# Keeping two engines in written order through the first block of seven products, with parameters, angles and the forget chain placed behind it

## The chip, the core and the metric

The kernel runs on one core of one Trainium2 chip. The metric is the device time of one execution in microseconds (us); smaller is better. An execution has five engines at work: TensorE (PE: matmuls, and PEld for its weight loads), VectorE (DVE), ScalarE (ACT), GpSimd (POOL) and SyncE (SP, which here only issues DMA transfers). Each engine carries out its own list of instructions in the order of the list and waits where an operand, a buffer or a transfer is not ready. Which instruction stands where in a list is therefore part of the program.

## What is computed

The reference is one decoder block on a sequence of 512 tokens and a width of 1024. One wide projection feeds two branches (an mLSTM matrix memory with 4 heads of 256, and a sparse attention with 8 heads of 64); their outputs are projected, merged by gates and projected once more.

```python
hN = _rmsnorm(x, norm_g[l])
p = _split_in(hN @ w_in[l])                      # 1024 x 8992, columns split by name
mq = silu(_causal_dwconv(p["m_q"], conv_q_w[l], conv_q_b[l]))
mk = silu(_causal_dwconv(p["m_k"], conv_k_w[l], conv_k_b[l]))
mh = _mlstm(mq, mk, p["m_v"], p["m_i"] + b_igate[l], p["m_f"] + b_fgate[l])
ya = sigmoid(p["m_o"]) * _head_layernorm(mh, mh_norm_g[l]) * silu(p["m_z"])
yn = _nsa(...)                                   # uses rope angles, compressed keys, gates
yb = yn * silu(p["n_z"])
merged = sigmoid(p["g_a"]) * (ya @ w_branch_a[l]) + sigmoid(p["g_b"]) * (yb @ w_branch_b[l])
x = x + merged @ w_out[l]
return _rmsnorm(x, final_norm_g)
```

The part that matters here is the early one: the columns `m_v`, `m_o` and `m_z` of the projection (1024 x 1024 each), the first columns of `g_a` and `g_b`, the small vectors (convolution weights, positions, compression positions), the rope angles (cosine and sine of the positions) and the logarithm of the forget gate.

## The kernel before

Every fp32 matmul is done in three fp32r matmuls: an operand is split into a high part (ACT, `A(hi, src, AF.Copy)`) and a low part (DVE, `lo = src - hi`), and the products hi·hi, hi·lo and lo·hi are added in PSUM. A split of one 128 x 1024 tile is one ACT pass and one DVE pass. All ACT and DVE instructions go through a helper and carry its line, L79, so they are told apart by tile names.

**Start.** The 512 tokens are normalised, transposed and split in four blocks of 128 into `hTh` and `hTl`. Each block is multiplied by a small set of columns (`last`, matmuls of L160 to L162), whose results `evacuate` takes out (`vsw`, `gp`).

**Seven products.** `winograd` computes a 1024 x 1024 projection in seven block products P1 to P7 rather than eight. A product is 24 matmuls of 128 x 512 (L482). The token side needs sums of blocks of `hTh + hTl`, which `token_sums` forms on DVE in the buffer `gate` and splits into the operands `S1` to `S4` (`S2h` and `S2l` for instance are the high and low part of `S2`). The weight side needs sums of quarter weights (`plus`: tiles `T`, from the loaded quarters `R`) and their splits (`hilo`: tiles `wh` and `wl`, four buffers each, handed from one split to the next when the matmuls that read them are done). The order of the products is P1, P2, P6, P7, P4, P5, P3. Results wait in `ka`, `kz`, `kw` (ACT copies) and are added on DVE by `finish` into the tiles `cq`. The block is run three times: for the columns `m_v`, `m_o` and `m_z`. `winograd` takes a table `between` of functions that are called after a named product.

**Jobs.** Between the products stand jobs of the `stream` object: 24 matmuls each (L202, L204, L206) that project 128 columns of `g_a` or `g_b`; ACT evacuates each into `sg`. In the first block four jobs run (J1 to J4 below). In the built order of before, J1 and J2 lie in among P1 and P2, J3 and J4 follow, then P6.

**Order.** The names in the set `ordered` are the engines whose instructions keep the order in which the code is written. The set holds ACT and DVE at the start, and `ordered.clear()` empties it right behind the evacuation of the fourth token block. From there on a scheduler places ACT and DVE instructions. Matmuls and transposes on PE are placed by the scheduler throughout.

**What stands behind `ordered.clear()`.** First the parameters (L398 to L417): eight small loads and one of 516 KB (`cst`), one POOL pass (`rotR`), and ten short PE transposes of `rows`, `crow` and `pf` into one bank, copied out by DVE as `prm`, `cpos` and the positions. Then the first `winograd` with `between` = one job and one step of `token_sums` after P1, three jobs and two steps after P2, and `angles` after P4. The function `angles` holds the angles (tiles `tiny`, a sine on ACT that needs its own table load, `cpad` and `spad`, eight PE transposes of L609 into `Ct` and `St`), the branch gates and the forget chain: a row of some 20 DVE instructions of 128 x 16 elements on `tiny`, each on the result of the one before, that ends in `lf` and `lfs`.

## Time and profile before

| what | value |
|---|---|
| time, median of 3 runs | 644.49 us (643.85 to 645.53) |
| the profiled execution's own time | 644.23 us |
| its span, first to last instruction | 642.4 us |
| PE busy | 613.9 us, 96% |
| DVE busy | 474.8 us, 74% |
| ACT busy | 335.4 us, 52% |
| mean granted TensorE clock | 0.991 |

The profile shows one execution. A row of the timeline gives the start and the length in us, the engine, the line, the operation, out<-in by tile names, and in square brackets the idle time of the engine just before, with the instruction that ended it. A row of the windows gives for a stretch A:B its length, and then for each engine the busy time and the number of instructions, the granted clock (1.00 is full speed), the share of time in which the DMA engines were busy, and GB/s. Matmul lengths overlap, since matmuls are pipelined: what one costs is the distance from one start to the next.

### The profile page before, as it was taken

What the parts mean: (1) busy time and instruction counts of PE and PEld (TensorE: products, weight loads), DVE (VectorE), ACT (ScalarE), POOL (GpSimd) and SP (SyncE); (2) the same over time, 40 slices, a digit from 0 to 9 for tenths busy, and PEclk for the clock granted to TensorE, in tenths of its full rate; (3) what the DMA queues carried; (4) which work ended last, traced back from release to release, by engine and by line L of the source; (5) the groups of instructions that cost most, each with busy time, mean ns of one, the idle gap of its engine ahead of it and who ended that gap; (6) DMA issues with size and microseconds to landing.
All of it is one profiled execution on the core that took longest, in us unless ns stands there. A gap on an engine that the chain in (4) does not pass through costs nothing.

```text
span 642.4 us, 8937 instructions
## 1 busy us (share of the span) xinstructions
PE 613.9 (96%) x3206; PEld 515.7 (80%) x3206; DVE 474.8 (74%) x938; ACT 335.4 (52%) x642; POOL 51.4 (8%) x114
## 2 busy tenths in 40 slices
PE   5977999999999999999999999999999999999995
PEld 3965887888888878887878877888888878888995
DVE  4999648779677577886876777789898987556444
ACT  5652554565443256566566575565656563234234
POOL 4100000000000002121212212000000000000000
PEclk9997999999999999999999999999999999999999
DMA  7942633622029453133032311622323254843103
GB/s 228 345 119 74 205 109 123 196 66 57 25 82 244 112 128 83 50 82 89 21 105 62 88 55 42 187 79 66 98 67 99 65 148 125 290 140 95 56 2 131
DMA packets 83659, 71.30 MB, mean 111 GB/s; under 512 B 4720, under 2 KB 68372, under 8 KB 83616
## 3 DMA queue, kind: packets, MB, share of 16 engines
q1 hardware_dynamic: 83616, 70.75, 37.0%
q8 instruction: 25, 0.41, 0.3%
q14 instruction: 18, 0.15, 0.1%
HBM read 61.30 MB, written 8.39 MB: 108 GB/s over the span
## 4 chain that ended last, share of the span: by engine, by line
PE 74%; DVE 16%; ACT 4%; issue 2%; DMA 2%; POOL 1%; SPq 0%; DVEq 0%; POOLq 0%; ACTq 0%
PE pp L204 12%; PE pp L202 12%; PE pp L206 12%; PE ps L482 9%; PE pt L482 4%; PE pp L162 3%; PE pp L482 3%; PE pp L161 3%; PE pp L160 3%; DVE wl L79 3%; DVE u L79 3%; PE pt L939 2%; PE po L952 1%; PE po L951 1%; ACT wh L79 1%
## 5 line engine op out<-in xcount | busy, mean ns | idle before, releaser
L202 PE MATMUL pp<-hTh,wh 128*128 128x512 f32 (+1 forms) x360 | 142.9, 397 | 0.0
L204 PE MATMUL pp<-hTl,wh 128*128 128x512 f32 (+1 forms) x360 | 140.3, 390 | 0.0
L206 PE MATMUL pp<-hTh,wl 128*128 128x512 f32 (+1 forms) x360 | 140.2, 389 | 0.0
L79 ACT ACTIVATE wh<-wr 128x1024 fp32r<-128x1024 f32 x64 | 67.5, 1058 | 75.4 <-PE pp L204 59.4
L79 DVE TENSOR_TENSOR wl<-wr,wh 128x1024 fp32r<-128x1024 f32 x64 | 77.9, 1218 | 14.1 <-ACT wh L79 14.1
L206 PEld LDWEIGHTS pp<-hTh,wl 128*128 128x128 f32 x360 | 67.9, 189 | 13.1
L202 PEld LDWEIGHTS pp<-hTh,wh 128*128 128x128 f32 x360 | 68.0, 189 | 10.5
L204 PEld LDWEIGHTS pp<-hTl,wh 128*128 128x128 f32 x360 | 68.1, 189 | 9.8
L933 POOL TENSOR_SCALAR P<-P,st 128x128 f32<-128x128 f32 (+1 forms) x64 | 34.4, 557 | 160.9 <-DVE st L79 69.0
L79 DVE TENSOR_TENSOR wl<-T,wh 128x1024 fp32r<-128x1024 f32 x24 | 29.3, 1223 | 19.9 <-ACT wh L79 19.9
L79 ACT ACTIVATE P<-P,st 128x128 f32<-128x128 f32 (+3 forms) x64 | 35.5, 556 | 11.2 <-DVE st L79 10.7
L79 DVE TENSOR_TENSOR ptl<-pt,pth 128x512 fp32r<-128x512 f32 (+1 forms) x64 | 29.9, 485 | 14.1 <-ACT pth L79 13.7
L79 ACT ACTIVATE pth<-pt 128x512 fp32r<-128x512 f32 (+1 forms) x64 | 26.9, 434 | 25.9 <-PE pt L939 14.5
L79 DVE CUSTOM_DVE_ANT_0 P<-ps,cst 128x128 f32<-128x128 f32 (+3 forms) x64 | 30.5, 487 | 12.7 <-PE ps L925 12.4
L161 PE MATMUL pp<-wl,meh 128*128 128x256 f32 x128 | 36.2, 283 | 0.0
L160 PE MATMUL pp<-wh,meh 128*128 128x256 f32 x128 | 36.2, 283 | 0.0
L162 PE MATMUL pp<-wh,mel 128*128 128x256 f32 x128 | 36.2, 284 | 0.0
L79 DVE SCALAR_TENSOR_TENSOR u<-pp,prm,u 128x511 f32<-128x511 f32 (+2 forms) x48 | 35.7, 744 | 0.2
L79 ACT ACTIVATE wh<-T 128x1024 fp32r<-128x1024 f32 x24 | 25.3, 1058 | 17.4 <-PE pp L204 6.5
L939 PE MATMUL pt<-cst,P 128*128 128x128 f32 x160 | 28.4, 277 | 0.9 <-DVE ptl L79 0.7
L939 PEld LDWEIGHTS pt<-cst,P 128*128 128x128 f32 x160 | 19.8, 141 | 10.8 <-DVE ptl L79 5.8
L79 DVE TENSOR_TENSOR wl<-R,wh 128x1024 fp32r<-128x1024 f32 x18 | 21.7, 1220 | 8.4 <-ACT wh L79 8.3
(324 smaller groups left out, 1410.9 us busy)
## 6 DMA issues: line engine op xcount, KB each, us to landing
wr<-w_in SPq DMA_DIRECT2D x44, 512.0 KB, 4.0
R<-w_in SPq DMA_DIRECT2D x24, 512.0 KB, 4.2
gD<-sg SPq DMA_DIRECT2D x16, 256.0 KB, 2.2
s<-gD SPq DMA_DIRECT2D x16, 256.0 KB, 5.2
wr<-w_branch_a SPq DMA_DIRECT2D x8, 512.0 KB, 3.8
wr<-w_out SPq DMA_DIRECT2D x8, 512.0 KB, 3.7
vD<-cq SPq DMA_DIRECT2D x8, 256.0 KB, 3.0
wr<-vD SPq DMA_DIRECT2D x4, 512.0 KB, 4.8
```

The costliest lines, as they stand in the source:

```text
L79: ins = fn(*args, **kw)
L160: pe.matmul(ps, a, c, start=start and i == 0, stop=False)
L161: pe.matmul(ps, a, d, start=False, stop=False)
L162: pe.matmul(ps, b, c, start=False, stop=stop and i == n - 1)
L202: pe.matmul(ps, a, c, start=k == 0, stop=False)
L204: pe.matmul(ps, a, d, start=False, stop=False)
L206: pe.matmul(ps, b, c, start=False, stop=k == nk - 1)
L482: m = lambda l, r, first=False, last=False: pe.matmul(banks[tb], l, r, start=first, stop=last, skip_group_check=True)
L933: pool.tensor_scalar(pj, pj, st[:, 2, j : j + 1], 1.0, OP.mult, OP.mult)
L939: pe.transpose(pt[:, (qb - kb) * 128 : (qb - kb) * 128 + 128], P[:, POFF[qb] + kb * 128 : POFF[qb] + kb * 128 + 128], ident,)
L951: pe.matmul(po[:, kb * 128 :], vl, th[:, :n], start=False, stop=False)
L952: pe.matmul(po[:, kb * 128 :], vl, tl[:, :n], start=False, stop=b == 1 and kb == 3)
```

## The change

The set `ordered` is no longer emptied behind the start but after P6 of the first block, so that ACT and DVE keep the written order through most of it, and the code is written in the order wanted. `hilo` moves out of `winograd`, and the weight split for P1 (`w1`) is written ahead of the first job's. The jobs and steps of the first block are called at new places of `winograd` (`t3`, `t2`, `C11`, `w6` beside the product names). The parameters become a generator `params`: its first part issues the loads, after the sum `t2`; its second part (the POOL pass, the transposes, the copies) runs after P7. Its tiles move: `rows` into the buffer `zt` of the third block, `crow` and `pi` into a wider `tiny`. `zt` is one tile of two halves where it was two buffers. `token_sums` forms its fourth sum one step earlier. `angles` stays behind P4. What is computed is the same.

```diff
         vq = quarters(vview, ((0, 0), (1, 0)))
+        w1 = hilo(vq[0, 0])
         stream.fetch()
         vq.update(quarters(vview, ((0, 1), (1, 1))))
         evacuate(NT - 1, last)
-        ordered.clear()
-
-        nc.sync.dma_start(cst[:, CROT:], consts[:, CROT:])
...
-        dve.tensor_copy(posT, ps[:, 128:132])
...
         t(c, b, c, OP.subtract)
+        t(d, c, hl("A12")[0], OP.add)
+        t(d, d, hl("A12")[1], OP.add)
         yield
         split(c, *parts["S2"])
         split(a, *parts["S3"])
         yield
-        t(d, c, hl("A12")[0], OP.add)
-        t(d, d, hl("A12")[1], OP.add)
         split(b, *parts["S1"])
         split(d, *parts["S4"])
...
-        product("P1", X, "A11", hilo(b11))
+        product("P1", X, "A11", w1 or hilo(b11))
+        do("P1")
         a = keep(X, "ka")
         Z = [PP() for _ in range(2)]
         w2 = hilo(b21)
         t3 = plus(WS(), b12, b22)
+        do("t3")
         t2 = plus(WS(), t3, b11)
+        do("t2")
         product("P2", Z, "A12", w2)
+        do("P2")
         finish(0, 0, Z, a, OP.add)
-        product("P6", X, "S2", hilo(t2), False)
+        do("C11")
+        w6 = hilo(t2)
+        do("w6")
+        product("P6", X, "S2", w6, False)
+        do("P6")
...
+    def params():
+        nc.sync.dma_start(cst[:, CROT:], consts[:, CROT:])
+        rows = wn.tile([128, D], F32, name="zt", tag="zt")[:11]
+        crow = tiny[:32, 384:512]
+        pi = tiny[:4, 512:640].bitcast(I32)
+        nc.sync.dma_start(pi, positions[0].rearrange("(a b) -> a b", a=4))
...
+        yield
+        pool.tensor_scalar(rotR, cst[:, CROT : CROT + 128], 1.0, 1.0, OP.mult, OP.mult)
+        ps = PP()
+        for k in range(8):
+            pe.transpose(ps[:, k * 11 : (k + 1) * 11], rows[:, k * 128 : (k + 1) * 128], ident[:11, :11])
...
+        pf = tiny[:4, 0:128]
+        dve.tensor_copy(pf, pi)
...
-    winograd(vq, staged, v_out, {"P1": (job, step), "P2": (job, step, job, step, job), "P4": (angles,)})
+    more = params()
+    load = lambda: next(more)
+    winograd(vq, staged, v_out, {
+        "P1": (step,), "t3": (job,), "t2": (job, load), "P2": (step,), "C11": (job, step),
+        "w6": (job,), "P6": (ordered.clear,), "P7": (lambda: next(more, None),), "P4": (angles,),
+    }, w1)
```

The built order shows what becomes of this. On PE the first block reads P1, J1, J2, P2, J3, J4, P6, P7, the parameter transposes, P4, P5 after the change. On ACT the copies `ka` and the split `wh` of P2 follow at once on P1; the sine and its table load, which stood ahead of P6's evacuation, stand between the two `wh` splits for P3.

DVE, from the end of the forget chain to the low split of P2's weights, before (`lf`, `lfs`: end of the chain; `prm`, `cpos`, `tiny`: parameters; `T`: weight sums; `wl<-wr`: a job's low split; `wl<-R`: P2's):

```order
L79 SCALAR_TENSOR_TENSOR lf<-gp,tiny 128x16
L79 TENSOR_TENSOR lfs<-lfs,lf 128x4 x2
L79 COPY prm<-pt 128x88
L79 COPY cpos<-pt 128x32
L79 TENSOR_SCALAR prm<-prm 128x8
L79 COPY tiny<-pt 128x4
L79 TENSOR_TENSOR T<-R 128x1024 x2
L79 TENSOR_TENSOR T<-T,R 128x1024
L79 TENSOR_TENSOR wl<-wr,wh 128x1024
L79 TENSOR_TENSOR wl<-R,wh 128x1024 x2
```

The same place now, from the last token sum (`gate`) on:

```order
L79 TENSOR_TENSOR gate<-gate,hTl 128x1024
L79 TENSOR_TENSOR wl<-R,wh 128x1024 x2
L79 TENSOR_TENSOR T<-R 128x1024 x2
L79 TENSOR_TENSOR wl<-wr,wh 128x1024
L79 TENSOR_TENSOR T<-T,R 128x1024 x2
L79 TENSOR_TENSOR wl<-wr,wh 128x1024
L79 TENSOR_TENSOR S2l<-gate,S2h 128x1024
L79 TENSOR_TENSOR S3l<-gate,S3h 128x1024
L79 TENSOR_TENSOR cq<-pp,ka 128x512 x2
L79 TENSOR_TENSOR tiny<-tiny 128x16
```

P2's low split stands right behind the token sums; eleven instructions of the forget chain follow only behind `cq`, still ahead of `S1l`, `S4l` and the low split for P6, and the rest of the chain comes later. Two of the eight sums on `gate`, which stood in among the token blocks of the start, are now in the row ahead of this place, and so is the cast of the loaded positions (`CAST tiny<-tiny 4x128`).

DVE at the end of the block, where the copies into `cpad` and `spad` (`cq<-tiny`) stand, and the results of P5 (`cq<-pt,kw`) are taken out. Before:

```order
L79 TENSOR_TENSOR wl<-R,wh 128x1024 x2
L79 TENSOR_TENSOR T<-R 128x1024
L79 TENSOR_TENSOR cq<-pt,kw 128x512
L79 TENSOR_TENSOR wl<-R,wh 128x1024
L79 TENSOR_TENSOR cq<-pt,kw 128x512
```

The same place now:

```order
L79 TENSOR_TENSOR wl<-R,wh 128x1024
L79 COPY cq<-tiny 128x4x8 x8
L79 TENSOR_TENSOR wl<-R,wh 128x1024
L79 TENSOR_TENSOR T<-R 128x1024
L79 TENSOR_TENSOR wl<-R,wh 128x1024
L79 TENSOR_TENSOR T<-R 128x1024
L79 TENSOR_TENSOR cq<-pt,kw 128x512 x2
```

Two sums `T<-R` of the second block, on freshly loaded quarters, now both stand ahead of `cq<-pt,kw`, and a low split of the second block between them.

PE at the same place, after P5 (`S1h`, `S1l`) and up to P3 (`S4h`, `S4l`); `ps` is the bank of the second block's P1. Before:

```order
L482 MATMUL pt<-wl,S1h 128x512
L482 MATMUL pt<-wh,S1l 128x512
L482 MATMUL pt<-wh,S4h 128x512
L482 MATMUL pt<-wl,S4h 128x512
L482 MATMUL pt<-wh,S4l 128x512
```

The same place now:

```order
L458 MATMUL pt<-wh,S1l 128x512
L458 MATMUL ps<-wh,hTh 128x512 x2
L458 MATMUL ps<-wl,hTh 128x512
L458 MATMUL ps<-wh,hTl 128x512
L458 MATMUL ps<-wh,hTh 128x512
L458 MATMUL ps<-wl,hTh 128x512
L458 MATMUL ps<-wh,hTl 128x512
L458 MATMUL ps<-wh,hTh 128x512
L458 MATMUL ps<-wl,hTh 128x512
L458 MATMUL ps<-wh,hTl 128x512
L458 MATMUL pt<-wh,S4h 128x512
```

Ten matmuls of the second block's P1 now stand ahead of the first block's P3. The eight transposes of L609 (`cq`), which stood between P4 and P5, stand after the ninth matmul of P5.

## The prediction

> **What bounds the kernel now.** I read the busy shares first, then the waits of PE, then the windows around the longest of them, and last the timelines of the two engines waited for.

> ```profile
> PE 613.9 (96%) x3206; PEld 515.7 (80%) x3206; DVE 474.8 (74%) x938; ACT 335.4 (52%) x642; POOL 51.4 (8%) x114
> PE pp L482 <- DVE wl L79: 4.0, 1, 4.0
> PE pp L482 <- ACT wh L79: 3.8, 1, 3.8
> PE pp L162 <- DVE hTl L79: 0.2, 1, 0.2
> PE ps L303 <- DMA grow<-norm_g: 4.5, 1, 4.5
> ```

> PE is busy for 96% of the span, so the end moves only by what PE waits or runs slowly. Two of its longest waits are single ones in the first block of products, both of P2, for the high and the low split of its weights.

> ```profile
> 30.81:41.74 10.93, 10.93 (x50) 8.77 (x48) 10.93 (x20) 3.92 (x8) 0.88 (x1) 1.00 0.31 91
> 41.74:46.39 4.65, 0.86 (x11) 0.69 (x10) 4.03 (x20) 4.46 (x7) 0.00 (x0) 1.00 0.62 165
> 46.39:52.81 6.42, 2.39 (x5) 1.38 (x5) 6.39 (x11) 3.73 (x4) 0.00 (x0) 0.51 0.33 87
> 52.81:56.39 3.58, 3.58 (x9) 2.81 (x9) 3.58 (x4) 0.00 (x0) 0.00 (x0) 0.50 0.56 148
> ...
> 41.51 0.39 PE L206 MATMUL pp<-hTh,wl 128*128 128x512 f32 x1
> 59.80 0.39 PE L202 MATMUL pp<-hTh,wh 128*128 128x512 f32 x1
> 75.44 0.39 PE L482 MATMUL ps<-wh,S2h 128*128 128x512 f32 x1
> ```

> Behind the first wait the granted clock (the column after POOL) falls to 0.51 and stays at 0.50 up to 56.39. From 59.80 to 75.44 lie 69 matmuls (the 21 left of J2, J3, J4): 15.64 / 69 = 0.2267 us each. J1 and P1 end at 41.51 + 0.23 = 41.74, and P6 begins at 75.44. Between lie P2, J2, J3 and J4, 96 matmuls or 21.76 us, in 33.70 us: **11.94 us are lost there**, by waiting and by the slow clock. That is all that this change can win at this place.

> ```profile
> 41.94 0.60 ACT L79 ACTIVATE sg<-pp 128x512 f32<-128x512 f32 x1 [7.14 <-PE pp L206]
> 43.38 1.07 ACT L79 ACTIVATE S2h<-gate 128x1024 fp32r<-128x1024 f32 x1
> 45.27 2.01 ACT L79 ACTIVATE wh<-R 128x1024 fp32r<-128x1024 f32 x2
> ...
> 42.67 0.17 DVE L79 TENSOR_SCALAR tiny<-tiny 128x16 f32<-128x16 f32 x1
> 42.88 0.18 DVE L79 TENSOR_TENSOR tiny<-tiny 128x16 f32<-128x16 f32 x1
> 46.99 2.36 DVE L79 TENSOR_TENSOR T<-R 128x1024 f32<-128x1024 f32 x2
> 51.54 2.35 DVE L79 TENSOR_TENSOR wl<-R,wh 128x1024 fp32r<-128x1024 f32 x2
> ```

> ACT was idle for 7.14 us until J1 ended, and then did `sg`, `ka`, `S2h` and a job's split before P2's `wh` at 45.27. DVE stood in the forget chain from 42.67 on (0.21 from one instruction to the next), then the parameters' copies and the sums `T`, before P2's `wl` at 51.54. Neither engine lacked time; both did other things first.

> **The change, part by part.** All times below are in the clock of this execution.

> PE up to P6: P1 can start at 30.81, where J1 started, if its split is ready.

> ```profile
> 28.61 2.00 ACT L79 ACTIVATE wh<-wr 128x1024 fp32r<-128x1024 f32 x2
> 33.78 1.21 DVE L79 TENSOR_TENSOR wl<-R,wh 128x1024 fp32r<-128x1024 f32 x1
> 34.92 1.31 DVE L79 TENSOR_TENSOR gate<-gate,hTh 128x1024 f32<-128x1024 f32 x1
> 62.00 1.28 DVE L79 TENSOR_TENSOR cq<-pp,ka 128x512 f32<-128x512 f32 x2
> ```

> ACT's first two splits run at 28.61 to 30.61, a DVE pass is 34.92 - 33.78 = 1.14 us, so P1's low splits end near 30.8 and 32.0; P1 needs them at 31.0 and 32.4. Then J1, J2, P2, J3, J4 follow without a break if DVE and ACT keep up: P2 at 30.81 + 72 x 0.2267 = 47.13, P6 at 30.81 + 144 x 0.2267 = 63.46.

> Does DVE keep up? Before, it came to its token sums at 34.92, behind four low splits and the last token block's small copies. The same stand ahead of them now, the splits in another order and the first not before ACT's at 29.7: I take 35.1. To P2's first low split stand eight sums, six small instructions (0.8 together, less than the 0.21 of the rows above for each, since they stand among passes and not on each other's results) and the pass itself: 35.1 + 9 x 1.14 + 0.8 = 46.2; P2's second matmul needs it at 47.4. Margin 1.2. To P6's second low split: 22 passes (25.1), the small ones (0.8), two `cq` (1.28), eleven of the forget chain (11 x 0.21 = 2.3): 35.1 + 29.5 = 64.6; needed by P6's eighth matmul at 65.05. Its first is done at 63.4 and needed at 63.69. Margin 0.3. So the forecast's wait here is 0; DVE 5% slower (1.5 us over this row) would cost 1.2. ACT has time: `wh` of P2 follows `ka` at 36.3 and is done near 39.5, and the three evacuations `sg` ahead of other splits cost 0.6 each where ACT waits for the job anyway.

> The loads: the positions that DVE casts now come behind a job's weights, which wait for the third low split (33.0), and `cst`.

> ```profile
> 25.72 0.41 SPq L402 DMA_DIRECT2D pi<-positions  x1
> 34.28 0.88 POOL L410 TENSOR_SCALAR rotR<-cst 128x128 fp32r<-128x128 f32 x1 [11.27 <-DMA cst<-consts]
> crow<-cmp_pos_k SPq DMA_DIRECT2D x1, 8.0 KB, 8.4
> ```

> SP issues them near 34.4. With ten large loads ahead, `cst` landed at 34.28 and `crow` took 8.4; now only two are ahead. By 8.4 they would land at 42.8, against the cast at 41.4: 1.4 late, of which P2's margin takes 1.2, but P6's only 0.3, so up to 1.1. By the load's median below (4.2) they are in time. I take 0, since the queue ahead is short.

> The parameter transposes move from a stretch in which PE waited anyway to a gap-free one between P7 and P4. Their cost was hidden; now it is open:

> ```profile
> 41.83 0.66 PE L413 MATMUL pt<-cst,rows 11*128 11x11 f32 x8
> 42.41 0.20 PE L417 MATMUL pt<-cst,pf 4*128 4x4 f32 x1
> ```

> From 41.74 to 42.61: 0.87 us. So P6, P7, transposes: P4 from 75.2 to 80.65. Their data landed long before (the last of these loads stands behind the store of J1's `sg`, near 44).

> The end of the block gets new waits.

> ```profile
> 69.56 0.26 ACT L79 ACTIVATE tiny<-tiny 128x64 f32<-128x64 f32 x1 [2.18 <-DVE tiny L79]
> 69.84 1.28 ACT L79 ACT_TABLE_LOAD   x1
> 71.13 0.60 ACT L79 ACTIVATE sg<-pp 128x512 f32<-128x512 f32 x1
> 69.91 0.80 DVE L79 COPY cq<-tiny 128x32 f32<-128x32 f32 x8 [0.38 <-ACT tiny L79]
> 91.77 1.03 PE L609 MATMUL pp<-cst,cq 128*128 128x128 f32 x8
> 98.69 0.50 PE L482 MATMUL pt<-wh,S4h 128*128 128x512 f32 x1 [0.44 <-DVE cq L79]
> DMA to landing us min/median/max: 3.8/4.2/4.4
> ```

> (1) ACT's first split for P3 waits for a buffer that P4 holds until six matmuls before its end (79.45); then 1.0 split, 1.28 table load, 0.26 sine, 0.8 DVE copies: 82.8. PE is at the transposes after nine matmuls of P5, at 82.7. Wait 0.2 with the hand-overs. (2) With 0.79 for the transposes, P5 ends at 87.1. The third of the ten matmuls ahead of P3 needs a low split that stands behind the first `T<-R`. That waits for a load (last row: 4.2 us) whose buffer is free after P3's first low split (81.6): 85.8, then two passes: 88.1. PE is there at 87.55: wait 0.55. (3) P3 itself waits for `cq`, behind the second `T<-R`, whose load starts at 84.1 and lands at 88.3; pass and `cq` end at 90.1; PE is there at 88.1 + 8 x 0.2267 = 89.9: wait 0.2. Together 0.95, between 0 (loads in 3.8, DVE a little ahead) and 1.5 (loads in 4.4, hand-overs of 0.1 each). Before, P3 waited 0.44 here (98.69). Net cost 0.5.

> [...] Here ACT goes on 0.01 us after the 1.28 of the load. [...]

> At the start, the token sums no longer stand in front of `hTl`, for which PE waited 0.2 (first fence): gain 0.2. The third block's `zt` as one tile of two halves, the wider `tiny` and the places of J3 and J4 change no count and no wait that PE has: nothing, and nothing hidden behind them. ACT has as many table loads. After the first block the lists are the same, and with PE full there the whole gain is carried to the end.

> **Sum.** 11.94 - 0.87 - 0.5 + 0.2 = **10.8 us**. The profiled execution took 644.23 (span 642.4 and 1.8 around it), 0.26 below the median of 644.49. 644.23 - 10.8 = **633.4 us**. Its own range: 632.2 (no new waits at the end: +0.95, and 0.3 less for the transposes) to 634.9 (margin at P6 missed by 0.9, waits of 1.5).

> **Rivals.**

> *DVE becomes the bound.* P6 stands 0.3 behind a row of 29.5 us on DVE. Rows 5% longer cost 1.2 at P6 and, with the angles late, up to 0.8 more: 635.4. For it: between 35 and 64 DVE has no slack. Against: the durations are those of the same instructions. 0.14.

> *The clock falls again.* Before, it fell behind a wait of 3.8 us. Three short waits within 8 us might do it too. Then 14 matmuls (5 and 9 in the two slow windows) at 0.43 and not 0.23 cost 2.8: 636.2. Against it:

> ```profile
> 92.00:110.00 18.00, 17.56 (x82) 14.34 (x81) 14.11 (x15) 8.97 (x12) 0.00 (x0) 1.00 0.45 146
> ```

> A wait of 0.44 left the clock at 1.00. 0.05. [...]

> [...] 0.03; it is the rule named above.

> *The positions land late*: 1.1 at P6, 634.5. 0.03.

> *Slower than before: P3 is held behind the next block's P1.* In PE's list ten matmuls stand ahead of P3 that hang on a load issued only after P3's own splits. Each us that the two loads land later than 4.2 is a us of PE, and past some 4 us of wait the slow clock adds 2.8. It decides from 8 + 2.8 = 10.8 us, a load of about 12 us; then 644.3 and up. The slowest small load took 8.4 with ten ahead, and these have one or two. 0.02.

> *The gain is not carried on*: a later wait on a transfer takes it back, 643 to 644. Against it, the only load in the list of PE's waits is the one of the start (`grow`, first fence). 0.03.

> **Chances.** The forecast 0.70, the rivals as given. About 0.3% (1.9 us) is what a measurement of this kernel can tell from no change. Faster by more: 0.95; within: 0.03; slower: 0.02. The range is the forecast's own, reaching up over the rivals of DVE, drain, positions and most of the clock: 632.2 to 636.0.

> **What would show it.** Right: no PE wait above 0.3 us from 30.8 to P4, granted clock 1.00 in every window from 30 to 60, P6 starting near 63.4, the ten transposes ahead of P4 at 74.3, waits of 0.2 to 0.6 at L629 and at the ten matmuls ahead of P3. Wrong: P6 starting after 65 with a wait on `wl` (DVE is the bound), a window under 1.00 between 80 and 95 (the clock), DVE idle before its cast near 41 (positions), P3 starting later than 92 (the loads).

## The result, and the profile after

| | before | after |
|---|---|---|
| time, median of 4 runs | 644.17 us (643.41 to 645.53) | 632.69 us (632.24 to 633.19) |
| the profiled execution, its span | 644.23, 642.4 | 633.19, 631.5 |
| mean granted TensorE clock | 0.991 | 0.997 |

The ratio is 0.982 (95% interval 0.9801 to 0.9838): 11.5 us less by the medians, 11.04 between the profiled executions. The forecast was 10.8 less, 633.4.

The busy shares of the page after: PE is busy 1.9 us less than before, in a span 10.9 shorter: the slow matmuls of before count as busy, its waits do not.

```profile
PE 612.0 (97%) x3206; PEld 514.7 (82%) x3206; DVE 474.6 (75%) x938; ACT 335.3 (53%) x642; POOL 50.2 (8%) x114
```

Of PE's waits these four lie at the start and in the first block. Both waits of P2 are gone, and two short ones are new: at the cosine and sine transposes (L629) and at the next block's P1 (L458).

```profile
PE ps L312 <- DMA grow<-norm_g: 3.9, 1, 3.9
PE pp L160 <- POOL v L342: 1.6, 1, 1.6
PE ps L458 <- DVE wl L79: 0.5, 1, 0.5
PE pp L629 <- DVE cq L79: 0.3, 1, 0.3
```

The windows of the same four stretches as before: PE (the second number) is busy all the time, and the granted clock is 1.00 where it was 1.00, 1.00, 0.51 and 0.50.

```profile
30.81:41.74 10.93, 10.93 (x49) 9.01 (x49) 10.59 (x18) 6.89 (x12) 0.45 (x1) 1.00 0.41 125
41.74:46.39 4.65, 4.65 (x22) 3.87 (x21) 4.65 (x7) 0.76 (x3) 0.00 (x0) 1.00 0.18 63
46.39:52.81 6.42, 6.42 (x30) 5.33 (x29) 6.42 (x7) 3.30 (x4) 0.00 (x0) 1.00 0.64 172
52.81:56.39 3.58, 3.58 (x17) 2.96 (x17) 3.58 (x5) 0.00 (x0) 0.00 (x0) 1.00 0.73 203
```

PE's timeline after: P1's first matmul, P2's first, P6's first two, then the parameters' transposes between P7 and P4, the two new waits and P3's start.

```profile
29.88 0.40 PE L458 MATMUL ps<-wh,hTh 128*128 128x512 f32 x1
...
46.27 0.39 PE L458 MATMUL pp<-wh,hTh 128*128 128x512 f32 x1
...
62.59 0.39 PE L458 MATMUL ps<-wh,S2h 128*128 128x512 f32 x1
62.82 0.40 PE L458 MATMUL ps<-wl,S2h 128*128 128x512 f32 x1
...
73.30 0.39 PE L458 MATMUL ps<-wh,S3l 128*128 128x512 f32 x1
73.62 0.66 PE L566 MATMUL pp<-cst,zt 11*128 11x11 f32 x8
...
74.67 0.40 PE L458 MATMUL ps<-wl,hTh 128*128 128x512 f32 x1
...
82.36 1.06 PE L629 MATMUL pp<-cst,cq 128*128 128x128 f32 x8 [0.26 <-DVE cq L79]
...
87.96 0.50 PE L458 MATMUL ps<-wl,hTh 128*128 128x512 f32 x1 [0.53 <-DVE wl L79]
...
89.91 0.40 PE L458 MATMUL pt<-wh,S4h 128*128 128x512 f32 x1
```

P6 stands 62.59 - 29.88 = 32.71 us behind P1: 144 matmuls at 0.227, with no break. DVE's rows show how narrow that is: P2's low splits, those for P6, and the two that the block's end hangs on.

```profile
44.23 2.35 DVE L79 TENSOR_TENSOR wl<-R,wh 128x1024 fp32r<-128x1024 f32 x2
...
61.42 4.63 DVE L79 TENSOR_TENSOR wl<-T,wh 128x1024 fp32r<-128x1024 f32 x4
...
84.75 1.23 DVE L79 TENSOR_TENSOR T<-R 128x1024 f32<-128x1024 f32 x1 [1.12 <-DMA R<-w_in]
86.68 1.23 DVE L79 TENSOR_TENSOR wl<-R,wh 128x1024 fp32r<-128x1024 f32 x1 [0.71 <-ACT wh L79]
```

One pass is 1.14. P2's first low split ends at 45.37 and is needed at 46.27 + 0.23 = 46.50: margin 1.1. P6's first ends at 62.56 and is needed at 62.82: margin 0.26.

**Two stretches** serve as a measure for all runs below: from the block's first matmul (J1 in before, P1 after) to P6's first, and from there to the first matmul of P6 in the third block, which has the same work in all of them (from each run's PE timeline, us). The times beside them are medians; each ratio is against before on the same chip.

| run | time | ratio, 95% | to P6 | P6 to third block |
|---|---|---|---|---|
| before | 644.17 | | 44.63 | 77.79 |
| after | 632.69 | 0.9801 to 0.9838 | 32.71 | 79.48 |
| e10, after once more | 633.19 | 0.9829 to 0.9859 | 32.72 | 79.40 |
| e1, order kept in before | 648.96 | 1.0062 to 1.0100 | 47.26 | 78.48 |
| e2, order not kept in after | 633.82 | 0.9836 to 0.9866 | 32.70 | 79.36 |
| e3, parameters in front | 642.19 | 0.9972 to 0.9990 | 44.25 | 77.57 |
| e4, the same, order not kept | 641.22 | 0.9948 to 0.9976 | 42.21 | 77.40 |
| e5, forget chain in front | 640.74 | 0.9950 to 0.9972 | 39.92 | 79.42 |
| e6, two passes more | 636.22 | 0.9867 to 0.9905 | 34.99 | 79.41 |
| e12, three passes more | 636.80 | 0.9883 to 0.9913 | 36.04 | 79.41 |
| e7, four passes more | 639.36 | 0.9923 to 0.9955 | 39.90 | 79.42 |
| e11, first job in front | 635.07 | 0.9860 to 0.9893 | 35.04 | 79.41 |
| e8, order kept to P7 | 640.94 | 0.9947 to 0.9972 | 32.71 | 87.32 |
| e9, parameters behind P6 | 631.84 | 0.9808 to 0.9837 | 32.72 | 78.20 |

After against before: 11.92 less to P6, 1.69 more behind it.

### The profile page after: what moved, and what is told of

Same layout as the page of the kernel before. It is cut to its first block, busy times and chain, and to the rows that moved or that the text cites. A ratio compares the mean times of both kernels' runs of the same rounds, so it can differ in the third digit from the quotient of the medians.

```text
span 631.5 us, 8947 instructions
## 1 busy us (share of the span) xinstructions
PE 612.0 (97%) x3206; PEld 514.7 (82%) x3206; DVE 474.6 (75%) x938; ACT 335.3 (53%) x642; POOL 50.2 (8%) x114
## 4 chain that ended last, share of the span: by engine, by line
PE 77%; DVE 13%; ACT 5%; issue 2%; POOL 1%; DMA 1%; SPq 0%; ACTq 0%; DVEq 0%; POOLq 0%
PE pp L204 12%; PE pp L202 12%; PE pp L206 12%; PE ps L458 10%; PE pt L458 4%; PE pp L162 3%; PE pp L160 3%; PE pp L161 3%; PE pp L458 3%; DVE u L79 3%; PE pt L964 2%; DVE wl L79 2%; ACT wh L79 1%; PE po L977 1%; PE po L976 1%
## 5 line engine op out<-in xcount | busy, mean ns | idle before, releaser
L202 PE MATMUL pp<-hTh,wh 128*128 128x512 f32 (+1 forms) x360 | 142.6, 396 | 0.0
L206 PE MATMUL pp<-hTh,wl 128*128 128x512 f32 (+1 forms) x360 | 139.8, 388 | 0.0
L79 ACT ACTIVATE wh<-wr 128x1024 fp32r<-128x1024 f32 x64 | 67.5, 1058 | 72.7 <-PE pp L204 64.4
L79 DVE TENSOR_TENSOR wl<-wr,wh 128x1024 fp32r<-128x1024 f32 x64 | 77.8, 1218 | 12.5 <-ACT wh L79 12.4
L206 PEld LDWEIGHTS pp<-hTh,wl 128*128 128x128 f32 x360 | 67.7, 188 | 13.1
L202 PEld LDWEIGHTS pp<-hTh,wh 128*128 128x128 f32 x360 | 67.8, 188 | 10.5
L958 POOL TENSOR_SCALAR P<-P,st 128x128 f32<-128x128 f32 (+1 forms) x64 | 34.4, 556 | 161.0 <-DVE st L79 69.1
L79 ACT ACTIVATE P<-P,st 128x128 f32<-128x128 f32 (+3 forms) x64 | 35.5, 555 | 11.2 <-DVE st L79 10.8
L79 DVE TENSOR_TENSOR ptl<-pt,pth 128x512 fp32r<-128x512 f32 (+1 forms) x64 | 29.9, 485 | 14.1 <-ACT pth L79 13.7
L79 ACT ACTIVATE pth<-pt 128x512 fp32r<-128x512 f32 (+1 forms) x64 | 26.8, 433 | 25.8 <-PE pt L964 14.4
L79 DVE CUSTOM_DVE_ANT_0 P<-ps,cst 128x128 f32<-128x128 f32 (+3 forms) x64 | 30.5, 487 | 12.7 <-PE ps L950 12.5
L79 DVE TENSOR_TENSOR wl<-T,wh 128x1024 fp32r<-128x1024 f32 x24 | 28.9, 1221 | 10.3 <-ACT wh L79 10.3
L162 PE MATMUL pp<-wh,mel 128*128 128x256 f32 x128 | 36.2, 284 | 0.0
L79 DVE SCALAR_TENSOR_TENSOR u<-pp,prm,u 128x511 f32<-128x511 f32 (+2 forms) x48 | 35.7, 743 | 0.2
L79 ACT ACTIVATE wh<-T 128x1024 fp32r<-128x1024 f32 x24 | 24.9, 1055 | 10.5 <-PE ps L458 5.6
L79 DVE TENSOR_TENSOR wl<-R,wh 128x1024 fp32r<-128x1024 f32 x18 | 21.7, 1221 | 9.8 <-ACT wh L79 9.7
L964 PEld LDWEIGHTS pt<-cst,P 128*128 128x128 f32 x160 | 19.7, 140 | 10.8 <-DVE ptl L79 5.8
```

Of the source, the lines that this page charges most:

```text
L79: ins = fn(*args, **kw)
L162: pe.matmul(ps, b, c, start=False, stop=stop and i == n - 1)
L202: pe.matmul(ps, a, c, start=k == 0, stop=False)
L206: pe.matmul(ps, b, c, start=False, stop=k == nk - 1)
L958: pool.tensor_scalar(pj, pj, st[:, 2, j : j + 1], 1.0, OP.mult, OP.mult)
L964: pe.transpose(pt[:, (qb - kb) * 128 : (qb - kb) * 128 + 128], P[:, POFF[qb] + kb * 128 : POFF[qb] + kb * 128 + 128], ident,)
```

## The experiments

The theory from the prediction: the 11.94 us were lost because DVE and ACT did other work ahead of P2's splits. What counts is then the work that stands there, whoever sets the order. Rivals: that the kept order is the cause (e1, e2, e8), or only one of the two things moved, parameters (e3, e4) or forget chain (e5).

### Is it the kept order? (e1, e2)

e1 is before with the set emptied later and nothing else:

```diff
-        ordered.clear()
...
-    {"P1": (job, step), "P2": (job, step, job, step, job), "P4": (angles,)}
+    {"P1": (job, step), "P2": (job, step, job, step, job), "P6": (ordered.clear,), "P4": (angles,)}
```

> Before's code, in which ScalarE and VectorE keep program order up to the end of P6, and nothing else is changed: parameters still in front of the block, J1 still ahead of P1. Theory: what costs the 11.94 us is what stands ahead of P2's splits, not who sets the order. In program order VectorE then stands at the cast of the positions and at the copies of the transposed parameters before its token sums, and ScalarE's splits for P2 and P6 come behind a job's. So PE waits several times before P6, 7 to 10 us in all, and the clock falls once or twice (2.8 each): 641 to 648, no faster than before by more than 3 us. Rival (kept order alone brings the gain): P2's two waits go and the time is 633 to 635.

It took 648.96, slower than before (1.0081) and 1 us above the expected range. DVE's rows of e1, and PE's row at P1's first low split:

```profile
40.43 0.56 DVE L79 TENSOR_TENSOR lfs<-lfs,lf 128x4 f32<-128x4 f32 x3
40.91 0.24 DVE L79 COPY prm<-pt 128x88 f32<-128x88 f32 x1
...
41.44 2.35 DVE L79 TENSOR_TENSOR wl<-R,wh 128x1024 fp32r<-128x1024 f32 x2
```

```profile
42.70 0.79 PE L481 MATMUL ps<-wl,hTh 128*128 128x512 f32 x1 [4.84 <-DVE wl L79]
```

Even P1's low split (41.44) now stands behind the copies of the parameters, and in front of those the scheduler has put the forget chain, which is not bound to the order. Kept order alone brings nothing.

e2 is the changed kernel with the set emptied at the old place:

```diff
         evacuate(NT - 1, last)
+        ordered.clear()
...
-        "w6": (job,), "P6": (ordered.clear,), "P7": (lambda: next(more, None),), "P4": (angles,),
+        "w6": (job,), "P7": (lambda: next(more, None),), "P4": (angles,),
```

> The changed kernel, but the two engines keep program order only up to where before gave it up: the scheduler is free in the whole block of seven products. Parameters, angles and forget chain stay behind it in the code. Theory: the place in the code brings the gain; P2 and P6 wait under 0.5, clock 1.00 from 30 to 60, time 631.5 to 634. Rival (the kept order brings it): the scheduler puts the forget chain and small work back ahead of P2's low split; a wait of 3 us or more at P2, a fall of the clock, 638 or more.

633.82, and 32.70 us to P6. The scheduler made another row (on DVE the cast of the positions at 62.04, where the changed kernel has it at 40.45, and the forget chain behind that), with the same result. So the kept order is not needed either: the place of the code is the cause. This has one limit: the forget chain's code stands behind P4 in both kernels, and only its place in the built row moved. The scheduler sets it early in before, e1 and e3, and late in after and e2; what it goes by is not shown.

### Which of the things moved? (e3, e4, e5)

e3 puts the parameters back in front of the block; e4 is the same with the order given up where before gave it up:

```diff
-    load = lambda: next(more)
+    next(more)
+    next(more, None)
...
-        "P1": (step,), "t3": (job,), "t2": (job, load), "P2": (step,), "C11": (job, step),
-        "w6": (job,), "P6": (ordered.clear,), "P7": (lambda: next(more, None),), "P4": (angles,),
+        "P1": (step,), "t3": (job,), "t2": (job,), "P2": (step,), "C11": (job, step),
+        "w6": (job,), "P6": (ordered.clear,), "P4": (angles,),
```

> The changed kernel with the parameters' loads, transposes and copies back in front of the block, program order kept, forget chain and angles behind it as changed. Theory: VectorE stands in its row at the copies of the parameters until their transposes are done, which PE has behind P1 (P1's 24 matmuls end near 36) and behind loads of about 8 us issued from 25 to 34; so its eight token sums start 5 to 8 us later than in the changed kernel, P2's low split is 4 to 7 late, the clock falls (2.8), and 0.87 of transposes comes off the gap-free stretch: 639 to 643. Rival (the parameters are only the 0.87 us of their transposes, the forget chain is the cause): within 1 us of the changed kernel, 631.8 to 633.5.

> As the run with the parameters in front, but with the scheduler free in the block (order kept only as far as before). Theory: the scheduler can put token sums and splits ahead of the copies, so VectorE does not stand at them, but jobs' weights come behind the parameters' loads and ScalarE's split for the second job behind the sums' splits: one wait of 3 to 7 us there and a fall of the clock if it is over some 3.8: 636 to 643. Rival (parameters cost only their transposes): 631.8 to 633.5.

Both times are in the theory's range (642.19, 641.22), by a mechanism that I had only half. The DVE rows of e3, then PE's last transpose and its wait in P2:

```profile
38.82 0.17 DVE L79 TENSOR_SCALAR tiny<-tiny 128x16 f32<-128x16 f32 x1 [2.89 <-ACT tiny L79]
...
43.76 0.24 DVE L79 COPY prm<-pp 128x88 f32<-128x88 f32 x1
...
44.29 1.21 DVE L79 TENSOR_TENSOR gate<-hTh,hTl 128x1024 f32<-128x1024 f32 x1
```

```profile
36.15 0.20 PE L570 MATMUL pp<-cst,tiny 4*128 4x4 f32 x1
...
55.55 0.80 PE L458 MATMUL pp<-wl,hTh 128*128 128x512 f32 x1 [7.87 <-DVE wl L79]
```

The transposes were done by 36.4, so DVE never stood at the copies for lack of data. In front of them stands, as in e1, the forget chain (38.82 to 43.8, after 2.89 us for its input from ACT), though the code has it behind P4 and it reads nothing of the parameters. The token sums start at 44.29 rather than 34.31, and P2 waits 7.87. In e4 the scheduler put the sums first, and the loss is on ACT, whose rows in e4 are:

```profile
46.91 1.28 ACT L79 ACT_TABLE_LOAD   x1
55.77 0.26 ACT L79 ACTIVATE tiny<-tiny 128x64 f32<-128x64 f32 x1 [7.58 <-DVE tiny L79]
...
58.29 0.60 ACT L79 ACTIVATE sg<-pp 128x512 f32<-128x512 f32 x1
```

The sine of the angles (55.77) has come ahead of a job's evacuation `sg`; ACT stands 7.58 us for its input, and PE 5.68 for `sg`. Parameters in front are thus not only 0.87 us of transposes: once they are early, small work from behind them comes early too (the chain in e3, the sine in e4), and holds the row in which it stands.

e5 moves the forget chain alone: its lines go out of `angles` into a function of their own, called behind P1 ahead of the token sums:

```diff
+    def forget():
+        A(gates, gp[:, :, 0:24], AF.Tanh, scale=0.5)
...
-        "P1": (step,), "t3": (job,), "t2": (job, load), "P2": (step,), "C11": (job, step),
+        "P1": (forget, step), "t3": (job,), "t2": (job, load), "P2": (step,), "C11": (job, step),
```

> The changed kernel with the gates' activations and the forget chain called right behind P1, ahead of the token sums, program order kept; parameters and angles stay where the change put them. Theory: some 26 small instructions, each on the result of the one before, of 0.21 us (5.4 us with what they wait of ScalarE at their start), stand ahead of P2's low split. Its margin is about 1.0, so P2 waits 3.5 to 4.5 there; the clock falls (2.8); the eleven small ones that now stand ahead of P6's split are gone, so P6 adds nothing: 638.5 to 640.5. If so long a wait leaves the clock up: 636 to 637.5. Rival (the parameters alone were the cause, the chain fits into gaps): 632 to 633.5.

640.74, just above the range; 7.2 us more to P6. PE's rows of e5:

```profile
48.17 0.50 PE L202 MATMUL pp<-hTh,wh 128*128 128x512 f32 x1 [0.95 <-ACT sg L79]
...
51.81 0.80 PE L458 MATMUL pp<-wl,hTh 128*128 128x512 f32 x1 [2.90 <-DVE wl L79]
```

The wait of about 4 is split: the scheduler set two matmuls of J3 ahead of the rest of P2, and they waited 0.95 for their bank, which J2 holds until ACT's `sg`. J4 then waits another 1.05 for `sg`. Against the rival, the chain alone costs most of the gain, and so do the parameters alone (which bring the chain with them). The two do not add: before had both and lost 11.9.

### How wide are the margins, and when does the clock fall? (e6, e12, e7, e11)

In e6, e12 and e7 one token sum is done three, four and five times: 2, 3 or 4 passes more ahead of P2's low split (in DVE's rows of e6 they start 1.26 us apart, each on the result of the one before; other passes take 1.14).

```diff
-        t(d, c, hl("A12")[0], OP.add)
+        for _ in range(3):
+            t(d, c, hl("A12")[0], OP.add)
```

> The changed kernel with one token sum done three times instead of once (the result is the same): two more passes of 1.14 us on VectorE ahead of P2's low split. By the margins of the traced run (P2's first low split done at 45.4, needed at 46.4; P6's done at 62.6, needed at 62.8): P2 waits 1.3, P6 0.7 to 0.9 more, clock 1.00 throughout: 2.0 to 2.3 us above the changed kernel, 634.5 to 635.2. Rival (short waits make the clock fall too): 637 to 638. Rival (VectorE has more slack than the rows say): under 633.5.

> Three more passes on VectorE ahead of P2's low split, between the runs with two (636.2, clock 1.00) and with four (639.4, clock down to 0.50 behind waits of 0.95 and 1.97 us). PE waits 0.95 for the third job and 0.8 for P2's low split, and 0.7 before P6. If the clock falls only when the idle time adds up to more than 2 us in 4: it stays at 1.00, 1.1 us above the run with two: 637.0 to 637.7. If it falls by then: 639 or more, no better than the run with four.

> As the run with two passes more, with four (4.56 us): P2 waits 3.5 to 3.7. Theory: a single wait of that length is what made the clock fall before (3.8 us there), so 14 to 16 matmuls at 0.43 us follow, 2.8 to 3.2 us; that gives VectorE its time back, so P6 does not wait: 6.3 to 7 us above the changed kernel, 639 to 640. If the clock stays up, P6 adds 0.8 and the sum is 4.3: 636.5 to 637.5.

To P6 they took 2.28, 3.33 and 7.19 more than the changed kernel: in size as forecast for e6 (2.0 to 2.3) and e12 (1.1 more than e6), and a little over for e7. But e6 does not wait where it was forecast: PE waited 0.95 for two matmuls of J3, which the scheduler set into P2, and 0.73 at J4's start, both for `sg`, and neither for P2's low split nor before P6. That its sum agrees is luck, and e6 does not measure the two margins. Its time was above its range (636.22; about 2.7 us over the changed kernel by the ratios of e6 and e10): in its profiled run some 0.8 lies in the landing of the last store (from the start of ACT's last instruction to the end of the span it is 5.1 us, and 4.3 after). e12's time (636.80) was 0.2 under its range. PE's rows of e12, then those of e7:

```profile
48.34 0.50 PE L202 MATMUL pp<-hTh,wh 128*128 128x512 f32 x1 [0.95 <-ACT sg L79]
...
49.78 0.50 PE L459 MATMUL pp<-wl,hTh 128*128 128x512 f32 x1 [0.70 <-DVE wl L79]
```

```profile
47.01 0.50 PE L202 MATMUL pp<-hTh,wh 128*128 128x512 f32 x1 [0.95 <-ACT sg L79]
...
49.71 0.79 PE L459 MATMUL pp<-wl,hTh 128*128 128x512 f32 x1 [1.97 <-DVE wl L79]
```

Behind 0.95 and 0.70 the clock stayed at 1.00; behind 0.95 and 1.97 it fell, and 7.19 - 3.33 - 1.26 = 2.6 us are its price (the prediction had 2.8).

e11 undoes another part: the first job stands ahead of the token sums again, as in before.

```diff
-        "P1": (step,), "t3": (job,), "t2": (job, load), "P2": (step,), "C11": (job, step),
+        "P1": (job, step), "t3": (), "t2": (job, load), "P2": (step,), "C11": (job, step),
```

> The changed kernel with its first job put back ahead of the token sums in the code, as before had it: J1's split of weights and its gate stand ahead of P1's evacuation on ScalarE, and one of J2's low splits (1.14 us) ahead of the token sums on VectorE. Theory: the margins are 1.0 at P2 and 0.3 at P6, and ScalarE now starts P2's high split behind J1's end, near 43.5, done by 45.5 (needed 46.3): one pass of 1.14 costs 0.2 at P2 and about 0.9 at P6, clock 1.00: 633 to 634.5. Rival (the job's place is what mattered on ScalarE: the wait of 3.8 for P2's high split comes back): 637 or more. Rival (no effect): under 632.9.

635.07, 1.9 above e10 on the same chip, and 2.3 more to P6: twice what I had expected. The token sums start 8.2 us behind P1's first matmul (4.4 in after), since DVE does not only one pass more but also waits 0.94 and 1.21 for ACT. PE waited 0.95 and 0.74 for `sg` at the starts of jobs, not at P2 or P6: the same two waits as in e6, at the same cost (2.28 there). The scheduler set matmuls of J3 into the rest of P2, as in e5 and e6, and their bank came late; the old wait of 3.8 for ACT did not come back. Two smaller parts of the change, P1's weight split ahead of the first job's and the fourth token sum one step earlier, were not undone by themselves.

### How far should the order be kept? (e8, e9)

e8 keeps it one product longer:

```diff
-        "P6": (ordered.clear,), "P7": (lambda: next(more, None),), "P4": (angles,),
+        "P7": (ordered.clear, lambda: next(more, None)), "P4": (angles,),
```

> The changed kernel with program order kept one product longer, to the end of P7's matmuls. Theory: order helps only as far as the code's order is the right one; in it both evacuations of P6 (kz) stand ahead of P7's splits, so ScalarE cannot split for P7 until P6 has ended, and PE waits about 0.6 + 1.0 for the high and 1.2 to 1.5 for the low split at P7, and more where the small instructions then crowd ahead of the next: 3 to 5 us above the changed kernel, 636 to 638. Rival (kept order is good as such): 632 to 633.

640.94: worse than expected. ACT's rows of e8, then PE's at P7:

```profile
68.12 0.60 ACT L79 ACTIVATE kz<-ps 128x512 f32<-128x512 f32 x1 [2.18 <-PE ps L458]
68.61 2.00 ACT L79 ACTIVATE wh<-T 128x1024 fp32r<-128x1024 f32 x2
```

```profile
69.72 0.73 PE L458 MATMUL ps<-wh,S3h 128*128 128x512 f32 x2 [0.98 <-ACT wh L79]
71.25 0.68 PE L458 MATMUL ps<-wl,S3h 128*128 128x512 f32 x1 [0.81 <-DVE wl L79]
```

P7's high split stands behind the evacuation `kz` of P6's second bank, as the code has it, and waits with it for P6's end. The mechanism is the one expected; the size was not, since the clock fell behind these waits (to 0.50 from 71.4 to 74.8) and again behind waits of 0.81 and 2.32 for the next block's P1.

e9 leaves the order as changed and does the parameters' transposes behind P6 instead of P7:

```diff
-        "P6": (ordered.clear,), "P7": (lambda: next(more, None),), "P4": (angles,),
+        "P6": (ordered.clear, lambda: next(more, None)), "P4": (angles,),
```

> The changed kernel with the parameters' transposes and copies one product earlier, between P6 and P7, and nothing else changed in the code. Theory: the 0.9 us of the transposes stays, but the angles then end earlier, so the sine comes ahead of both splits for P3, the cos and sin transposes stand earlier among P5's matmuls, and only two of the next block's P1 matmuls stand ahead of P3, so the wait of 0.53 in front of the third (0.92 with the refill) goes; a wait of 0.2 to 0.4 at P3 and at the cos and sin transposes is left. 0.3 to 0.9 us less than the changed kernel: 631.8 to 632.4 where that gives 632.7. Rival (small copies now crowd ahead of P7's split, as where order was kept to P7): 633 to 635.

> The changed kernel once more, unchanged, to compare with the run that moves the parameters ahead of P7: 632.2 to 633.2 by its four runs; P1 from 29.5 to 30.5, P6 32.7 after it, no wait of PE between them.

631.84 against 633.19 for the changed kernel on the same chip: each of four runs (631.24 to 632.07) is below each of the other four (632.62 to 633.54), and behind P6 it is 1.20 us less, more than the 0.3 to 0.9 expected. PE's rows of e9 at the transposes and at P3, then ACT's at the sine:

```profile
80.21 1.03 PE L629 MATMUL pp<-cst,cq 128*128 128x128 f32 x8
...
86.88 0.46 PE L458 MATMUL pt<-wh,S4h 128*128 128x512 f32 x1
```

```profile
78.20 0.26 ACT L79 ACTIVATE tiny<-tiny 128x64 f32<-128x64 f32 x1 [0.56 <-DVE tiny L79]
```

The sine comes 3 us earlier (78.20, after: 81.16), and neither new wait is left, nor the 0.2 to 0.4 that was expected to stay. It is the fastest version measured, though only by 0.2%, and the two ratios' intervals overlap.

## Why the prediction was right, step by step

- **The loss of 11.94 us**: 44.63 to 32.71 is 11.92. Right, and e3 and e5 show that it comes back with the work in front.
- **DVE keeps up** (margins 1.2 and 0.3): 1.1 and 0.26. Right. The rival of DVE as the bound was 0.3 us away. What overstepping costs is shown less directly: in e6 and e11 PE pays in waits for `sg`, and only the third and fourth pass more (e12, e7) show up as a longer wait for P2's low split, by 0.70 and 1.26.
- **Positions in time**: the cast at 40.45 waited for nothing. Right.
- **Transposes, 0.87**: P7's last matmul starts at 73.30, the second of P4 at 74.67; without them they would be two matmuls apart. 1.37 - 0.45 = 0.92.
- **New waits at the block's end, net 0.5**: this step was mis-sized. Its first wait (forecast 0.2) is 0.26, its second (0.55) 0.53, its third (0.2) didn't come. But on PE's path each of these waits cost more than its bracket. In the timeline, start to start less 0.2267 a matmul, the 0.53 cost 0.92, the 0.26 cost 0.47 (the eight transposes took 1.36 with it, 0.89 in before without), and before's 0.44 at P3 cost 0.70. Net 0.69. Also, the second wait's cause was not the load, as the step had it, so that its size came out near 0.55 is luck: `T<-R` was done at 85.9, and the low split then waited 0.71 for ACT's high split (quoted above). ACT's row of that split after, then in e9:

```profile
85.59 1.06 ACT L79 ACTIVATE wh<-R 128x1024 fp32r<-128x1024 f32 x1 [0.49 <-ACT cq L79]
```

```profile
85.19 1.06 ACT L79 ACTIVATE wh<-R 128x1024 fp32r<-128x1024 f32 x1 [1.97 <-issue]
```

ACT was idle before it in both, and in both began it 1.1 us before P5 ended (86.70, in e9 86.31). By the code this split takes the buffer of P5's first weight tile (there are four, used in turn), and P5 reads that tile up to six matmuls before its end: 85.34 after and 84.95 in e9, about 0.25 before the split. The instruction that the first bracket names had ended at 85.10, so it is not what the split waited for. From 85.34 on, one high and one low split (1.06 and 1.23) end long after the second of the ten matmuls. So by this account the third waits however early its load lands, unless P3 stands ahead of it, as in e9.

- **The start, 0.2**: P1 began at 29.88, 0.93 ahead of before's J1. That can't be put down to the change: the twelve other profiled runs have their first block matmul between 28.99 and 30.38, and the wait for `hTl` that the step removed is there in e6 and e7 (0.2). It stays open how much of the 0.93 is the change's.
- **The table load**: the prediction takes its row as it stands, and its range reaches up over a drain behind it, as long again (chance 0.03). No run shows such a drain. ACT's rows after:

```profile
79.87 1.28 ACT L79 ACT_TABLE_LOAD   x1
81.16 0.26 ACT L79 ACTIVATE tiny<-tiny 128x64 f32<-128x64 f32 x1
```

79.87 + 1.28 is 81.15, and the sine starts at 81.16: 0.01, as in before; in e10, e11 and e12 it starts 0.01 to 0.02 behind its load.

- **The other rivals**: the clock stayed at 1.00 behind the short waits (every window above, and up to 110 us), though in e7 and e8 it fell behind waits under 2 us (0.95 and 1.97, 0.98 and 0.81; last section), and P3, which a late load might have held, started at 89.91; its load held DVE for 1.12 (quoted above).
- **The gain is carried to the end**: from the third block's P6 to the end of the span are 642.4 - 153.23 = 489.2 before and 631.5 - 142.07 = 489.4 after. Right.

In sum: 11.92 - 0.92 - 0.69 = 10.31 (the stretches give 11.92 - 1.69 = 10.23), 0.93 from the start, 0.26 given back behind the third block: 10.9 of span, where the forecast had 10.8 by a better end and a smaller start. The main term, 11.94, was understood; that the total is so close is in part luck, since the 0.73 more at the start, whose cause is open, covers 0.32 more at the block's end and the 0.26.

## What to carry to other kernels

Look at what stands in an engine's row ahead of the split that PE waits for, and move small dependent chains and one-off copies behind it; whether a scheduler or the written order then makes the row matters little (e2), while a kept order around a badly placed row costs time (e1, e8). Parameters made available early also brought other small work forward: the sine, which hangs on them (e4), and the forget chain, which does not (e3). So after such a move read the whole built row, not only what was moved. The three waits of PE taken apart above cost 0.2 to 0.4 us more than their brackets (0.47 for 0.26, 0.70 for 0.44, 0.92 for 0.53), and several close together cost the clock too where PE was busy for 1.66 us or less in a window of 3.41 (next section).

## What was not expected of the hardware

**In these traces the slow clock lasts 3.41 us or a multiple of it.** Windows of 0.4 us around the fall and the rise, in e5 and then in e7 (the number after POOL is the mean clock):

```profile
51.20:51.60 0.40, 0.00 (x0) 0.00 (x0) 0.40 (x1) 0.00 (x0) 0.00 (x0) 0.87 1.15 348
54.80:55.20 0.40, 0.40 (x3) 0.28 (x3) 0.40 (x2) 0.00 (x0) 0.00 (x0) 0.86 0.00 0
```

```profile
48.40:48.80 0.40, 0.00 (x0) 0.00 (x0) 0.40 (x2) 0.40 (x1) 0.00 (x0) 0.68 0.98 245
55.20:55.60 0.40, 0.40 (x2) 0.31 (x2) 0.40 (x2) 0.00 (x0) 0.00 (x0) 0.79 0.65 61
```

Between 1.00 and 0.50, a mean of 0.87 says that the fall was at 51.50, and 0.86 that the rise was at 54.91: 3.41 us. In e7 it is 48.54 to 55.37, 6.83, twice that; read in the same way, before has 46.54 to 56.78, three times that. Waits under 2 us were enough: the clock fell behind 0.95 and 1.97 us in e7, and behind 0.98 and 0.81, with the ten transposes just ahead, in e8; it did not behind 0.95 and 0.70 in e12.

**The clock fell behind windows in which PE was busy for 1.66 us or less.** The clock's changes lie whole windows of 3.4133 us apart (in before, read in windows of 0.1 and 0.2 us, the falls at 46.55 and 640.46 are 593.91 us apart, 174 windows), so the windows can be placed in each run, and PE's busy time (the second number) read in each. e7's fall at 48.54 ends a window; in e1 the rise at 47.57 lies 8 windows before 74.87; in e12 the fall at the kernel's end, at 632.10, lies 171 windows behind 48.42. One window of e7, one of e1, and two of e12:

```profile
45.13:48.54 3.41, 1.66 (x7) 0.72 (x5) 3.41 (x6) 3.13 (x4) 0.00 (x0) 1.00 0.21 65
74.87:78.28 3.41, 1.73 (x7) 0.82 (x5) 1.27 (x2) 2.30 (x3) 1.05 (x2) 1.00 0.62 231
45.01:48.42 3.41, 2.46 (x12) 1.72 (x10) 3.41 (x5) 1.67 (x3) 0.00 (x0) 1.00 0.00 0
48.42:51.83 3.41, 2.71 (x11) 1.90 (x12) 3.41 (x4) 1.77 (x2) 0.00 (x0) 1.00 0.76 210
```

The other thing is what a wait of PE cost beyond its bracket: 0.21, 0.26 and 0.39 us for waits of 0.26, 0.44 and 0.53, worked out above at the block's end.
